# The opening of a two-layer DiT block on one core: who issues the loads, and where the modulation chunks and weight splits stand

## The chip, the cores and the metric

The kernel runs on one core of a Trainium2 chip. The metric is device time in microseconds (us) of one execution; the median of the runs is compared. The core has several engines that run side by side and are held together by semaphores: PE (TensorE, matrix products), DVE (VectorE), ACT (ScalarE), POOL (GpSimd) and SP (SyncE, which here only issues transfers). Sixteen DMA engines move the data. SBUF is the on-chip memory, PSUM holds the results of PE.

## The reference

What is computed is a block of two transformer layers on a sequence `x` (512 tokens of 1024 values) with a context `ctx` (256 tokens), all in fp32. The parts that matter here are those at the very beginning, the modulation and the first layer's mixer:

```python
for i in range(DEPTH):                      # DEPTH = 2
    sh1, sc1, g1, sh2, sc2, g2 = _adaln(c, w_mod[i], b_mod[i])      # silu(c) @ w_mod + b_mod
    hx = _modulate(_rms_norm(x, norm1[i]), sh1, sc1)                # h * (1 + scale) + shift
    # the same for ctx, with c_ctx
    if i == 0:
        yx = _fourier_hyena_mixer(hx, *fh)                          # begins with  proj = h @ w_in
        yc = _fourier_hyena_mixer(hc, *fh)
    else:
        yx = ...                                                    # attention over x and ctx
    x = x + g1 * yx
    x = x + g2 * _conv_ffn(_modulate(_rms_norm(x, norm2[i]), sh2, sc2), *ffn)
```

with

```python
def _rms_norm(x, g):
    y = x32 * lax.rsqrt(jnp.mean(x32 * x32, axis=-1, keepdims=True) + EPS)
    return y * g
```

The mixer also needs a small filter network, three layers of `h = sin(freq * (h @ w + b))`, which depends on no token and is calculated in the opening too.

## The kernel before

All activations are kept transposed: a row tile `x[d]` (d = 0 to 7) holds 128 of the 1024 values on the partitions, and along them 512 tokens of `x` and 256 of `ctx`. A matrix product in fp32 is made of three products of a shorter type: each factor is split into a high part (`hi`, a copy on ACT, L133) and a low part (`lo`, a subtraction on DVE, L138), and `mm3` (L158 to L160) issues high by high, high by low and low by high. A weight tile of 512 KB has its parts `wr` (raw), `wh` and `wl`; a row tile of the normalised input has `hh` and `hl`.

The opening is the part up to the end of the first three projections, about 72 us long. Its order on PE, DVE, SP and ACT is the order in which the code is written (a block in which the scheduler leaves these four engines alone). It has these pieces:

- **Loads**, all issued by SP: the table of columns `pcol` (L189), the constants `cst` (L191), the conditions `cT` (L198), the filter's `zT` and `fw` (L403, L404), eight tiles of `x` of 256 KB (L460), eight of the context of 128 KB (L462), then the modulation's weights `wm`, two chunks of 2 x 1 MB (L209), and three tiles of `w_in` (L146). There are only so many DMA semaphores, so an issue further back can wait for the landing of an earlier load.
- **Silu** of the conditions on ACT (L201), which brings a load of ACT's function table, into `sT`.
- **Sums of squares**: `s1(d)` and `s2(d)` for x and the context, a square on ACT (L267) and an addition on DVE (L274). `f1(True, 0)` and `f2(True, 0)` sum over the partitions with PE (`fold`, L280), scale on DVE (`nrm_s`, L285) and take the reciprocal root in 11 small DVE operations (L167 to L176). `f1(True, 1)` and `f2(True, 1)` spread the result over all partitions with PE (L298) and copy it out on ACT (L301).
- **Modulation chunks**: four chunks of 512 outputs of shift and scale. `gemv_pe` multiplies `sT` with a chunk of weights in 8 matmuls of PE (L219) and copies the result on ACT (L222); the function that it returns, called `turn` below, brings it onto the partitions with four matmuls (L227) and adds the bias on DVE (L232). Chunks 0 and 1 cover the row tiles 0 to 3, chunks 2 and 3 the row tiles 4 to 7. `make_A` (L251) makes of the scale the factor A. The pool of `wm` has two buffers.
- **The filter network**: a matmul (L410), the argument's reduction on DVE (`sine`, L384 to L393) and Sin on ACT (L414).
- **Spare matmuls** (`spare`, L470): products whose result nobody reads, that fill waits of PE.
- **Row tiles**: `both(d, 0)` multiplies x by A and by the root for x and for the context (L308, DVE) and adds the shift (L309, ACT), which gives `hh`; `both(d, 1)` gives `hl` (L313, DVE).
- **Products**: `first(m, k)` is the share of row tile k in projection m, six matmuls. The results of three projections grow side by side in PSUM (`ps3`). After the first four row tiles come the others, one after another, each with three products.

All small results of PE (`ms`) share two PSUM buffers: the fold's, the spreading's, the chunks' and the filter's matmuls all write a buffer of this pair, so that each must wait until the one before the last has been read. From the taps (L616) on nothing is changed.

Of the kernel before, what the change touches and what calls it, by code (L numbers as in the profile page):

```python
# [22 lines left out]
C = 256  # L23
C0 = 514
# [61 lines left out]
class Builder:  # L86
# [94 lines left out]
    def setup(self):  # L181
        nc, I = self.nc, self.I
        self.P0 = self.pool("P0")
        self.W = self.pool("W", bufs=3)
        self.ps = self.pool("psA", space=PSUM)
        self.sm = self.pool("sm", bufs=2)
        p = self.P0
        self.pcol = self.t(p, [P, NCOLS], F32, "pcol")
        nc.sync.dma_start(self.pcol, I["pcol"])  # L189
        cst = self.t(p, [P, 132], F32, "cst")  # L190
        nc.sync.dma_start(cst, I["cst"])  # L191
        self.ident, self.e4, self.sel, self.alt = cst[:, 0:128], cst[:, 128:129], cst[:, 129:131], cst[:, 131:132]
        self.ones32 = self.t(p, [P, 32], F32, "ones32")
        nc.vector.memset(self.ones32, 1.0)
        self.mod = [self.t(p, [P, 48, 2], F32, f"mod{i}") for i in range(2)]
        self.A = [[self.t(p, [P, 2, 8], F32, f"A{i}{k}") for k in range(2)] for i in range(2)]
        cT = self.t(p, [P, KD, 2], F32, "cT")
        nc.sync.dma_start(cT, I["cT"])  # L198
        self.sT = self.t(p, [P, KD, 32], F32, "sT")
        nc.vector.memset(self.sT, 0.0)  # L200
        nc.scalar.activation(self.sT[:, :, 0:2], cT, AF.Silu)  # L201
        self.sbp = self.pool("sbp", side="right")
        self.sb = self.t(self.sbp, [P, 2, D], F32, "sb")

# [191 lines left out]
    def filter_mlp(self):  # L396
# [3 lines left out]
        zT = self.t(p, [66, 384], F32, "zT")  # L400
        fw = self.t(p, [P, 3, P], F32, "fw")
        self.w4 = self.t(p, [P, 1024], F32, "w4")
        nc.sync.dma_start(zT, I["zT"])  # L403
        nc.sync.dma_start(fw, I["fw"])  # L404

        def layer(l, h, step):
            if step == 0:
# [25 lines left out]
    def mixer(self):  # L433
# [21 lines left out]
        with self.tc.manual_schedule(engines={ENG.PE, ENG.DVE, ENG.SP, ENG.Activation}):  # L455
# [3 lines left out]
            for d in range(KD):  # L459
                nc.sync.dma_start(x[d][:, 0:512], I["xT"][d])  # L460
            for d in range(KD):
                nc.sync.dma_start(x[d][:, C0 : C0 + C], I["cxT"][d])  # L462
            wm = [self.gemv_raw(0), self.gemv_raw(1)]
            win = [self.wraw(I["w_in"][m]) for m in range(3)]
            ps3 = [self.mm() for _ in range(3)]
# [10 lines left out]
            for d in range(KD):  # L476
                s2(d)
            f1(True, 0)
            spare(5)
            f2(True, 0)  # L480
            spare(3)
            f1(True, 1)
            g0 = self.gemv_pe(0, 0, wm[0])
            wm.append(self.gemv_raw(2))
            f2(True, 1)
            h = layer(0, layer(0, pa, 1), 2)
            g0()
            spare(3)
            wins = [self.wsplit(win[0])]
            g1 = self.gemv_pe(0, 1, wm[1])  # L490
            spare(1)
            wm.append(self.gemv_raw(3))
            nc.sync.dma_start(self.w4, I["w4"])
            for tt in (4, 5):
                dec[tt] = tp()
                nc.sync.dma_start(dec[tt], I["decay"][tt])
            wins.append(self.wsplit(win[1]))
            g1()
            self.make_A(0, 0, b=4)
            for d in range(KD):  # L500
                hh.append(self.t(hp, [P, TW], F32R, f"hh{d}"))
# [10 lines left out]
                self.proj_k(ps3[m], wins[m], hh, hl, k)  # L512

            pa = layer(1, h, 0)
            spare(5)
            both(0, 0)
            both(1, 0)
            both(0, 1)
            first(0, 0)
            first(1, 0)  # L520
            wins.append(self.wsplit(win[2]))
            both(1, 1)
            both(2, 0)
            first(0, 1)
            first(1, 1)
            both(3, 0)
            both(2, 1)
            first(2, 0)
            first(2, 1)
            g2 = self.gemv_pe(0, 2, wm[2])  # L530
            both(3, 1)
            h = layer(1, layer(1, pa, 1), 2)
            first(0, 2)
            g2()
            first(1, 2)
            first(2, 2)
            g3 = self.gemv_pe(0, 3, wm[3])
            first(0, 3)
            g3()
            self.make_A(0, 0, a=4)  # L540
            first(1, 3)
            first(2, 3)
            self.close("wm")
            self.pg = self.pool("pg")
# [1398 lines left out]
```

## Time and profile before

| what | us |
|---|---|
| median of 3 runs | 1628.01 (1627.53 to 1628.06) |
| the profiled execution, its own time | 1633.3 |
| its span, first to last instruction | 1631.5 |
| busy PE in the span | 1589.6 (97%) |
| busy DVE, ACT | 1048.2 (64%), 620.1 (38%) |
| mean granted clock of PE | 0.991 |
| the first square (L267) starts at | 6.32 |
| the first product of a row tile starts at | 37.31 |
| the first matmul that reads `hl` of row tile 4 starts at | 59.28 |
| the taps (L616) begin at | 72.56 |

The profile is of one execution. A row of a timeline has the start, the time to the end of the group in us, the engine, the line, the operation, what goes out and in, and how many instructions are in the group; in square brackets stands how long the engine was idle before it and what it waited for. A row of the stages has the stretch, its length, and the busy time of each engine with its number of instructions; then the granted clock of PE (1.00 is full speed), the share of the DMA engines' time that was taken, and GB/s. A row of the chain of waits has start, length and what ran. fp32 matmuls that are not split are counted twice in the timeline.

### The profile page before, as it was taken

The page shows a single profiled execution, that of the slowest core. Times are in us where ns is not written, and L with a number is a line of the kernel's source. Part 1 is how long each engine was busy: PE and PEld are TensorE (multiplying, and loading weights), DVE is VectorE, ACT ScalarE, POOL GpSimd, SP SyncE. Part 2 cuts the span into 40 slices and gives each one's busy share as a digit, 9 for nine tenths or more (in the row PEclk, how much of TensorE's full clock was granted, in tenths as well). Part 3 has the DMA queues.
Part 4 walks back from the last instruction along what each step waited for, and adds up shares of the span by engine and source line. Part 5 has one row for each costly group of instructions (what it writes and reads, how often), then busy time and mean ns, then how long its engine had stood idle before and what let it go on. Part 6 is the DMA issues. An engine that isn't in the chain of part 4 may idle for free.

```text
span 1631.5 us, 20800 instructions
## 1 busy us (share of the span) xinstructions
PE 1589.6 (97%) x8248; PEld 1300.2 (80%) x8248; DVE 1048.2 (64%) x1702; ACT 620.1 (38%) x883; POOL 109.5 (7%) x165
## 2 busy tenths in 40 slices
PE   7999998999999999999999999999989999999999
PEld 5687888888888888888888887566559888888887
DVE  5788869878786354643354577899977544344243
ACT  4451224424222212222133337898953432233131
POOL 0112134000000000000000001121210000000000
PEclk9999998999999999999999999999999999999999
DMA  9336412533443243432342210000033232222222
GB/s 344 108 117 211 170 36 72 194 117 106 166 155 129 66 141 129 159 125 71 108 147 99 95 55 16 13 11 13 0 129 116 78 103 102 80 104 98 83 91 90
DMA packets 54542, 173.35 MB, mean 106 GB/s; under 512 B 6188, under 2 KB 9454, under 8 KB 53422
## 3 DMA queue, kind: packets, MB, share of 16 engines
q1 hardware_dynamic: 54445, 172.03, 30.5%
q8 instruction: 65, 1.06, 0.3%
q14 instruction: 32, 0.25, 0.0%
HBM read 166.24 MB, written 5.77 MB: 105 GB/s over the span
## 4 chain that ended last, share of the span: by engine, by line
PE 81%; DVE 13%; DMA 2%; issue 2%; ACT 1%; POOL 1%; SPq 0%; POOLq 0%; ACTq 0%; DVEq 0%
PE mm L158 24%; PE mm L159 23%; PE mm L160 23%; PE pv L1613 2%; DVE junk L243 2%; DVE S L1589 1%; DVE wl L138 1%; PE s L1559 1%; DVE wr L1628 1%; DMA wr<-w_in 1%; PE k L158 1%; PE k L159 1%; PE k L160 1%; DMA wm<-wmod0a 1%; PE mm L616 1%
## 5 line engine op out<-in xcount | busy, mean ns | idle before, releaser
L158 PE MATMUL mm<-hh,wh 128*128 128x512 f32 (+2 forms) x1360 | 480.9, 356 | 1.8 <-ACT wh L133 0.9
L159 PE MATMUL mm<-hl,wh 128*128 128x512 f32 (+2 forms) x1360 | 478.6, 353 | 2.3 <-DVE hl L313 2.3
L160 PE MATMUL mm<-hh,wl 128*128 128x512 f32 (+2 forms) x1360 | 478.4, 352 | 1.6 <-DVE wl L138 1.6
L133 ACT ACTIVATE wh<-wr 128x1024 fp32r<-128x1024 f32 (+1 forms) x192 | 197.8, 1033 | 579.8 <-PE mm L159 544.6
L138 DVE TENSOR_TENSOR wl<-wr,wh 128x1024 fp32r<-128x1024 f32 (+2 forms) x192 | 231.2, 1207 | 234.9 <-ACT wh L133 228.3
L158 PEld LDWEIGHTS mm<-hh,wh 128*128 128x128 f32 x1360 | 256.6, 189 | 48.4 <-issue 7.6
L159 PEld LDWEIGHTS mm<-hl,wh 128*128 128x128 f32 x1360 | 257.1, 189 | 39.2 <-DVE hl L313 3.5
L160 PEld LDWEIGHTS mm<-hh,wl 128*128 128x128 f32 x1360 | 256.9, 189 | 37.5 <-DVE wl L138 2.2
L243 DVE SCALAR_TENSOR_TENSOR junk<-wr,sb 128x1024 bf16<-128x1024 f32 x128 | 156.2, 1220 | 41.2 <-DMA wr<-wmodT 40.7
L158 PE MATMUL mm<-ah,wh 128*128 128x512 f32 (+1 forms) x480 | 172.4, 359 | 0.0
L160 PE MATMUL mm<-ah,wl 128*128 128x512 f32 (+1 forms) x480 | 172.2, 359 | 0.0
L159 PE MATMUL mm<-al,wh 128*128 128x512 f32 (+1 forms) x480 | 171.9, 359 | 0.0
L1143 DVE SCALAR_TENSOR_TENSOR xr<-mm,mod,xr 128x512 f32<-128x512 f32 (+1 forms) x100 | 61.8, 632 | 160.6 <-PE mm L160 160.1
L159 PEld LDWEIGHTS mm<-al,wh 128*128 128x128 f32 x480 | 90.5, 189 | 14.2 <-DVE al L138 0.2
L158 PEld LDWEIGHTS mm<-ah,wh 128*128 128x128 f32 x480 | 90.4, 188 | 14.1 <-issue 0.3
L160 PEld LDWEIGHTS mm<-ah,wl 128*128 128x128 f32 x480 | 90.4, 188 | 14.2
L1613 PE MATMUL pv<-S,V 128*128 128x512 f32 x192 | 93.9, 598 | 2.5 <-ACT S L1592 2.5
L1175 ACT ACTIVATE fg<-fg 128x772 f32<-128x772 f32 (+1 forms) x44 | 32.6, 741 | 98.0 <-DVE fg L375 91.4
L1567 ACT ACTIVATE S<-s,rks 128x512 f32<-128x512 f32 x96 | 62.6, 685 | 12.4 <-PE pv L1613 8.5
L1613 PEld LDWEIGHTS pv<-S,V 128*128 128x128 f32 x192 | 34.5, 190 | 34.7 <-issue 29.3
L1589 DVE TENSOR_TENSOR S<-S,mx 128x1536 f32<-128x1536 f32 x32 | 55.4, 1750 | 2.3 <-POOL mx L1585 2.3
L1585 POOL PARTITION_ALL_REDUCE mx<-mx x16 | 44.9, 2806 | 161.6 <-DVE mx L1582 161.6
(337 smaller groups left out, 2273.2 us busy)
## 6 DMA issues: line engine op xcount, KB each, us to landing
wr<-w_up SPq DMA_DIRECT2D x88, 512.0 KB, 3.2
wr<-wmodT SPq DMA_DIRECT2D x80, 512.0 KB, 3.2
wr<-w_dn SPq DMA_DIRECT2D x32, 512.0 KB, 3.2
wm<-wmod0a SPq DMA_DIRECT2D x8, 1024.0 KB, 8.9
wr<-w_in SPq DMA_DIRECT2D x16, 512.0 KB, 4.2
wr<-w_out SPq DMA_DIRECT2D x13, 512.0 KB, 3.7
wr<-w_dn SPq DMA_DIRECT2D x17, 384.0 KB, 3.0
wr<-w_o SPq DMA_DIRECT2D x11, 512.0 KB, 3.2
```

Source lines behind the costliest of these rows:

```text
L133: self.nc.scalar.activation(dst, src, AF.Copy)
L138: (eng or self.nc.vector).tensor_tensor(dst, src, hi.bitcast(F32), op=ALU.subtract)
L158: mmul(out, wh, xh, start=start, stop=False)
L159: mmul(out, wh, xl, start=False, stop=False)
L160: mmul(out, wl, xh, start=False, stop=stop)
L243: nc.vector.scalar_tensor_tensor(junk, raw, 1.0, self.sb[:, j, :], op0=ALU.mult, op1=ALU.mult, accum_out=acc)
L1143: nc.vector.scalar_tensor_tensor(x[m][:, a2:b2], ps[:, a2:b2], mod[:, 8 * sec + m, c : c + 1], x[m][:, a2:b2], op0=ALU.mult, op1=ALU.add)
L1175: nc.scalar.activation(g[:, :n], g[:, :n], AF.Silu)
L1567: nc.scalar.activation(c.S[a][j // 3][:, j % 3, :], c.ps[a, j], AF.Copy, scale=c.r[:, g : g + 1])
L1585: nc.gpsimd.partition_all_reduce(c.m[a][:, 1, :], c.m[a][:, 0, :], P, bass.bass_isa.ReduceOp.max)
L1589: v.tensor_tensor(c.S[a][h], c.S[a][h], mb.to_broadcast([P, 3, T]), op=ALU.subtract)
L1613: nc.tensor.matmul(c.P[a], V[:, j, o : o + 128], c.S[a][j // 3][:, j % 3, :], start=j == 0, stop=j == 5)
```

## The change

Three things are changed, all in the opening; what is computed is the same.

First, `pcol`, `zT`, `fw` and the eight context tiles are issued by ACT instead of SP, 11 of the loads, and Silu is moved behind these 11 issues. Second, on PE the modulation chunks 0 and 1 are put between the folds and spreadings, with fewer spare matmuls. Third, only the first weight is split ahead of the row tiles; the second and third are split behind row tiles 0 and 2, the row tiles are normalised one by one, and the products are in another order.

```diff
-        nc.sync.dma_start(self.pcol, I["pcol"])
+        nc.scalar.dma_start(self.pcol, I["pcol"])
...
-        nc.scalar.activation(self.sT[:, :, 0:2], cT, AF.Silu)
+        self.cT = cT
...
-        nc.sync.dma_start(zT, I["zT"])
-        nc.sync.dma_start(fw, I["fw"])
+        nc.scalar.dma_start(zT, I["zT"])
+        nc.scalar.dma_start(fw, I["fw"])
...
             for d in range(KD):
-                nc.sync.dma_start(x[d][:, C0 : C0 + C], I["cxT"][d])
+                nc.scalar.dma_start(x[d][:, C0 : C0 + C], I["cxT"][d])
+            nc.scalar.activation(self.sT[:, :, 0:2], self.cT, AF.Silu)
...
             f1(True, 0)
-            spare(5)
-            f2(True, 0)
-            spare(3)
-            f1(True, 1)
+            spare(2)
             g0 = self.gemv_pe(0, 0, wm[0])
             wm.append(self.gemv_raw(2))
+            f1(True, 1)
+            f2(True, 0)
+            g0()
+            g1 = self.gemv_pe(0, 1, wm[1])
+            wm.append(self.gemv_raw(3))
             f2(True, 1)
             h = layer(0, layer(0, pa, 1), 2)
-            g0()
-            spare(3)
+            g1()
             wins = [self.wsplit(win[0])]
-            g1 = self.gemv_pe(0, 1, wm[1])
-            spare(1)
-            wm.append(self.gemv_raw(3))
...
-            wins.append(self.wsplit(win[1]))
-            g1()
             self.make_A(0, 0, b=4)
...
             pa = layer(1, h, 0)
-            spare(5)
+            spare(3)
             both(0, 0)
+            both(0, 1)
+            wins.append(self.wsplit(win[1]))
             both(1, 0)
-            both(0, 1)
             first(0, 0)
+            both(1, 1)
             first(1, 0)
-            wins.append(self.wsplit(win[2]))
-            both(1, 1)
             both(2, 0)
             first(0, 1)
             first(1, 1)
+            both(2, 1)
+            wins.append(self.wsplit(win[2]))
+            first(0, 2)
+            first(1, 2)
             both(3, 0)
-            both(2, 1)
             first(2, 0)
             first(2, 1)
             g2 = self.gemv_pe(0, 2, wm[2])
             both(3, 1)
             h = layer(1, layer(1, pa, 1), 2)
-            first(0, 2)
+            first(2, 2)
             g2()
-            first(1, 2)
-            first(2, 2)
+            first(0, 3)
             g3 = self.gemv_pe(0, 3, wm[3])
-            first(0, 3)
+            first(1, 3)
             g3()
             self.make_A(0, 0, a=4)
-            first(1, 3)
             first(2, 3)
```

The order of the instructions on ACT at its very beginning, before (the numbers behind names tell instances of a tile apart; `s_38` is the first square):

```order
L201 ACT_TABLE_LOAD
L201 ACTIVATE sT_81<-cT_79 128x8x2
L267 ACTIVATE s_38_168<-x_16_109 128x512
L267 ACTIVATE s_39_170<-x_17_110 128x512
L267 ACTIVATE s_40_173<-x_18_111 128x512
```

and now:

```order
L189 DMA pcol_67<-pcol 128x360
L403 DMA zT_119<-zT 66x384
L404 DMA fw_120<-fw 128x384
L462 DMA x_16_108<-cxT 128x256
L462 DMA x_17_109<-cxT 128x256
L462 DMA x_18_110<-cxT 128x256
L462 DMA x_19_111<-cxT 128x256
L462 DMA x_20_112<-cxT 128x256
L462 DMA x_21_113<-cxT 128x256
L462 DMA x_22_114<-cxT 128x256
L462 DMA x_23_115<-cxT 128x256
L463 ACT_TABLE_LOAD
```

Eleven issues stand ahead of the table's load, Silu and the first square.

On PE, from the fold of x (L280 with four columns) to the second chunk's turn (the second L227), before:

```order
L280 MATMUL ms_214<-ones_3_71,s_38_168 128x1 x4
L470 MATMUL mm_157<-s_28_125,cst_69 128x256 x5
L280 MATMUL ms_248<-ones_3_71,s_46_191 128x1 x2
L470 MATMUL mm_157<-s_28_125,cst_69 128x256 x3
L298 MATMUL ms_278<-cst_69,rq_r_241 128x128 x4
L219 MATMUL ms_285<-wm_143,sT_81 32x512 x8
L298 MATMUL ms_299<-cst_69,rq_r_273 128x128 x2
L227 MATMUL ms_314<-cst_69,s_83_294 128x2 x4
L470 MATMUL mm_157<-s_28_125,cst_69 128x256 x3
L219 MATMUL ms_327<-wm_146,sT_81 32x512 x8
L470 MATMUL mm_157<-s_28_125,cst_69 128x256
L227 MATMUL ms_351<-cst_69,s_93_336 128x2 x4
```

and now:

```order
L280 MATMUL ms_214<-ones_3_71,s_38_168 128x1 x4
L471 MATMUL mm_157<-s_28_124,cst_69 128x256 x2
L219 MATMUL ms_245<-wm_143,sT_81 32x512 x8
L298 MATMUL ms_259<-cst_69,rq_r_241 128x128 x4
L280 MATMUL ms_266<-ones_3_71,s_46_191 128x1 x2
L227 MATMUL ms_293<-cst_69,s_68_254 128x2 x4
L219 MATMUL ms_299<-wm_146,sT_81 32x512 x8
L298 MATMUL ms_313<-cst_69,rq_r_291 128x128 x2
L227 MATMUL ms_328<-cst_69,s_87_308 128x2 x4
```

The first chunk comes ahead of the spreading of x, the fold of the context behind that, and no spare matmul stands between the first chunk and the second chunk's turn.

On DVE, from chunk 0's bias (the first L232) to the first row tiles, before:

```order
L232 TENSOR_TENSOR mod_4_73<-ms_314,pcol_67 128x8
L138 TENSOR_TENSOR wl_324<-wr_149,wh_323 128x1024
L138 TENSOR_TENSOR wl_348<-wr_151,wh_347 128x1024
L232 TENSOR_TENSOR mod_4_73<-ms_351,pcol_67 128x8
L251 SCALAR_TENSOR_TENSOR A_6_75<-mod_4_73,pcol_67 128x4 x2
L308 SCALAR_TENSOR_TENSOR s_117_414<-x_16_109,A_6_75,s_81_283 128x512
```

and now:

```order
L232 TENSOR_TENSOR mod_4_73<-ms_328,pcol_67 128x8
L138 TENSOR_TENSOR wl_335<-wr_149,wh_334 128x1024
L251 SCALAR_TENSOR_TENSOR A_6_75<-mod_4_73,pcol_67 128x4 x2
L308 SCALAR_TENSOR_TENSOR s_115_398<-x_16_108,A_6_75,s_71_264 128x512
L308 SCALAR_TENSOR_TENSOR s_116_401<-x_16_108,A_6_75,s_90_316 128x256
L313 SCALAR_TENSOR_TENSOR hl_99_346<-s_115_398,mod_4_73,hh_98_345 128x512
L313 SCALAR_TENSOR_TENSOR hl_99_346<-s_116_401,mod_4_73,hh_98_345 128x256
L138 TENSOR_TENSOR wl_407<-wr_151,wh_406 128x1024
```

The low part of the second weight stands behind the first row tile instead of ahead of it; the first L232 of the second listing is that of chunk 1, and chunk 0's now stands ahead of the filter's `sine`.

## The prediction

> **What bounds the kernel now.** I read the page's head first, then the busy time by stage, then the chain of waits through the opening, and last the timelines of PE, DVE and ACT with the granted clock beside them.
>
> ```profile
> span 1631.5 us, 20800 instructions
> PE 1589.6 (97%) x8248; PEld 1300.2 (80%) x8248; DVE 1048.2 (64%) x1702; ACT 620.1 (38%) x883; POOL 109.5 (7%) x165
> ```
>
> PE is busy for 97% of the span, so 42 us of idle PE are all that any ordering can win. The stages (columns: length, busy PE, PEld, DVE, ACT, POOL, granted clock, DMA share, GB/s) say how much of that lies where the change acts:
>
> ```profile
> 0.00:37.30 37.30, 28.17 (x126) 20.05 (x126) 20.13 (x60) 14.59 (x27) 1.20 (x36) 0.91 0.92 340
> 37.30:59.30 22.00, 19.67 (x122) 14.08 (x122) 16.30 (x32) 8.41 (x15) 4.31 (x2) 1.00 0.62 226
> 59.30:72.50 13.20, 13.20 (x73) 11.34 (x73) 9.05 (x18) 5.02 (x9) 0.00 (x0) 1.00 0.13 40
> ```
>
> The last of them is solid: 13.20 of 13.20 us. The change leaves it as it is, so the whole question is when it begins, that is when the first matmul with hl4 (the low part of row tile 4) starts, 59.28 us before. Every microsecond by which that instant moves is taken over by the span. The chain of waits up to the first product:
>
> ```profile
> 6.30 6.12 DMA x<-xT
> 12.44 1.25 ACT s L267 x3
> ...
> 16.12 4.48 PE mm L470 x10
> ...
> 23.77 0.59 ACT s L301
> ```
>
> The data come first, then squares and sums, then PE. The 4.48 us of L470 are spare matmuls; they lie on this chain because fold and spread stand behind them; then comes the first copy of a spreading, 0.59.
>
> **The loads.** Before, SP issues everything, and ACT starts its squares when x0 lands. The rows are, in this order, ACT's timeline, SP's timeline, the loads by kind (size, median us to landing), the tile x, and the waits of SP's queue:
>
> ```profile
> 3.94 1.28 ACT L201 ACT_TABLE_LOAD   x1 [3.94 <-DMA cT<-cT]
> 5.23 0.22 ACT L201 ACTIVATE sT<-cT 128x16 f32<-128x16 f32 x1
> 6.32 0.63 ACT L267 ACTIVATE s<-x 128x512 f32<-128x512 f32 x1 [0.87 <-DMA x<-xT]
> ...
> 1.17 0.42 SPq L191 DMA_DIRECT2D cst<-cst  x1
> ...
> cT<-cT SPq DMA_DIRECT2D x1, 8.0 KB, 2.2
> ...
> x<-cxT SPq DMA_DIRECT2D x8, 128.0 KB, 4.2
> ...
> DMA to landing us min/median/max: 3.0/4.8/6.1
> ...
> SPq L462 <- DMA x<-xT: 2.6, 7, 0.7
> ```
>
> Afterwards 11 issues stand on ACT ahead of its table load, Silu and squares. The last row says that issues wait for earlier landings (here 7 times): a load is let out only when the one whose place it takes has landed. In the built program the ACT issue of cx2 (the third context tile's load) waits for cT, and that of cx7 for cx2. cT is now SP's second load, issued when cst was (1.17), so it lands at 1.17 + 2.2 = 3.4. cx2 goes out by 3.7, lands 4.2 later at 7.9, cx7's issue ends by 8.25, and table load and Silu (1.28 + 0.22) come after that. The first square starts at 9.75 instead of 6.32. With the fastest and slowest landing of an x load (3.0 and 6.1, the row with minimum, median and maximum) it is 8.55 or 11.6. The issue time saved on SP (11 issues at about 0.4) buys nothing here, since the queue that needs the data waits behind its own issues.
>
> The Trainium skill's "DMA: Bandwidth & Descriptors", section "Issuing engines are not separate DMA queues", says that issuing from several engines saves only the sequencer's issue time, the transfers sharing the same 16 DMA engines. The trace agrees: 0.92 of the DMA engines' time is taken over the whole first stage.
>
> **Sums.** By 9.75 most tiles have landed, so from there DVE sets the pace:
>
> ```profile
> 9.72 8.19 DVE L274 TENSOR_TENSOR s<-s,s 128x512 f32<-128x512 f32 x13 [0.31 <-ACT s L267]
> 17.83 0.15 DVE L285 TENSOR_SCALAR nrm_s<-ms 128x4 f32<-128x4 f32 x1
> ...
> 20.00 0.16 DVE L176 SCALAR_TENSOR_TENSOR rq_r<-rq_b,rq_r 128x4 f32<-128x4 f32 x1
> ```
>
> The first add can start when two squares are done (0.63 each, overlapping a little), about 10.94, the second some 0.8 later at 11.74. The other 13, as the row has them, took 8.11 us to the next instruction (9.72 to 17.83), so nrm_s of x starts at about 19.85 instead of 17.83: two microseconds late. If DVE ran them closer together, gemv 0 (the first modulation chunk) would still have to wait for its 2 MB: up to the end of that chunk 5.8 MB are to be moved, and the 340 GB/s of the first stage, with a start near 3 us, give 17 + 3 = 20 us. The reciprocal root takes 2.33 us as before (17.83 to 20.16).
>
> **The chunks between sums and spreadings.** These rows price the new order (x16 is 8 matmuls of the program, each twice):
>
> ```profile
> 22.68 1.05 PE L298 MATMUL ms<-cst,rq_r 128*128 128x128 f32 x8
> 24.41 1.92 PE L219 MATMUL ms<-wm,sT 128*32 128x512 f32 x16 [0.67 <-ACT s L301]
> ...
> 27.04 0.71 PE L298 MATMUL ms<-cst,rq_r 128*128 128x128 f32 x4 [0.70 <-ACT s L222]
> 28.21 1.05 PE L227 MATMUL ms<-cst,s 128*128 128x2 f32 x8 [0.46 <-ACT s L301]
> ...
> 24.44 0.67 DVE L384 TENSOR_SCALAR s<-ms,pcol 128x384 f32<-128x384 f32 x1
> ...
> 27.71 0.36 DVE L393 TENSOR_SCALAR s<-s 128x384 f32<-128x384 f32 x1
> ...
> 29.67 1.23 DVE L138 TENSOR_TENSOR wl<-wr,wh 128x1024 fp32r<-128x1024 f32 x1 [0.20 <-ACT wh L133]
> ...
> 35.75 2.21 DVE L308 SCALAR_TENSOR_TENSOR s<-x,A,s 128x512 f32<-128x512 f32 x4
> ...
> 37.31 0.49 PE L158 MATMUL mm<-hh,wh 128*128 128x512 f32 x1
> ```
>
> ms, the PSUM tile that all these matmuls write, has two buffers, so each of these steps waits for the reader of the last but one. gemv 0 waits for nrm_s of x: 20.05 to 21.97. Its copy lasts 0.6; spread x (1.05) stands behind it, 22.7 to 23.7; fold c waits for spread x's copy, 24.4 to 24.95 (four matmuls that I price a little under the 0.71 of spread c). DVE's root for c ends at 27.3 and chunk 0's addition at 27.5; only that frees the buffer for gemv 1, 27.5 to 29.5. Copy, spread c (0.71), copy, and turn 1 (1.05) reach 32.4. Behind DVE's sine (3.63 before, from 24.44 to the end of L393 at 28.07) comes wh of weight 0, to 32.85, and wl of weight 0 (1.23), to 34.1; A is ready at 34.5. From the start of L308 to the first product it was 1.56 us (35.75 to 37.31), so the first product comes at 36.2: **1.1 us earlier**, in spite of the two lost at the front. The gain is that the second weight's split and 12 of the 25 spares are off the path.
>
> **Projections.** The splits that were ahead are now between row tiles, on DVE:
>
> ```profile
> 39.59 0.40 PE L158 MATMUL mm<-hh,wh 128*128 128x512 f32 x1
> ...
> 40.65 0.39 PE L158 MATMUL mm<-hh,wh 128*128 128x512 f32 x1
> ...
> 45.82 1.92 PE L219 MATMUL ms<-wm,sT 128*32 128x512 f32 x16
> ...
> 54.97 0.95 PE L227 MATMUL ms<-cst,s 128*128 128x2 f32 x8
> ...
> 59.28 0.50 PE L159 MATMUL mm<-hl,wh 128*128 128x512 f32 x1 [0.86 <-DVE hl L313]
> ```
>
> One product (six matmuls) is 39.59 to 40.65, 1.06 us. On DVE, each pair of L308 is about 1.1 (2.21 for two), each pair of L313, of the same shape, is taken at as much, and wl of weight 1 is 1.23; three row tiles need 34.6 + 6 x 1.1 + 1.23 and some waits for ACT's hh, and the first six products end near 45.1 instead of just before 45.82 (-0.75). From there to chunk 3's turn stand five products instead of four: +1.06. The turn comes at 55.2 (54.97 before), and hl4's first matmul 4.31 later, as now: 59.6. **At full clock the sum is +0.3 us.** That turn now has one product behind it instead of two, so PE's stall there grows by 1.06.
>
> **The clock.** The granted clock is where I expect the rest (PE's wait before fold x, and stretches with the same columns as the stages):
>
> ```profile
> 14.45 1.67 PE L280 MATMUL ms<-ones,s 128*128 128x1 f32 x8 [1.91 <-DVE s L274]
> ...
> 11.30:14.70 3.40, 1.49 (x9) 1.01 (x7) 3.07 (x5) 3.31 (x9) 0.00 (x0) 1.00 0.98 313
> 14.70:18.10 3.40, 3.40 (x13) 3.04 (x13) 2.74 (x9) 1.10 (x3) 0.00 (x0) 0.50 0.93 355
> 57.00:60.40 3.40, 2.54 (x14) 2.00 (x13) 3.40 (x8) 2.74 (x6) 0.00 (x0) 1.00 0.00 0
> 188.80:192.20 3.40, 1.51 (x10) 1.22 (x10) 2.48 (x6) 1.38 (x2) 1.57 (x2) 1.00 0.42 154
> 192.20:195.60 3.40, 3.40 (x13) 2.93 (x12) 3.37 (x7) 1.36 (x2) 0.00 (x0) 0.50 0.19 42
> ```
>
> Two stretches of 3.4 us in which PE was busy for 1.49 and 1.51 us are each followed by one at half the clock, though PE was wholly busy there; after 2.54 it stays at 1.00, as the solid stage from 59.30 on shows. Somewhere between lies the point at which it is lost. Three places fall under it now. (a) Spares end near 12.5 (14.45 - 1.91), fold x is at 16.5: idle 3.9 us where it was 1.9, and only 2 spares follow instead of 5 before the next wait. The clock is lost as before, but gemv 0 (1.92) comes while it may still be away: between 0 and 1.9, I take 1.0, half of it. (b) Between gemv 0's end and gemv 1's start PE works 1.05 + 0.55 + 1.0 = 2.6 of 5.5 us, a share of 47%, against 44% in the two stretches that lost it and 75% in the one that kept it. At half clock gemv 1 costs 1.9 more, spread c 0.5, turn 1 0.65: 0 to 3.05, I take 1.0, since a stretch may end between them. (c) At chunk 3's stall busy falls from 2.54 to 2.54 - 1.06 = 1.5, as in the two stretches that lost it; a solid stretch of 3.4 us at half the clock does 1.7 us less work: 0 to 1.7, I take 1.7, as the row at 192.20 shows. Sum: 0.3 + 1.0 + 1.0 + 1.7 = **+4.0 us**.
>
> The Trainium skill's "TensorE: Matmul & The Clock Gate", section "Why this matters for your kernels", asks for no idle gaps of PE over about 3 us and says that one idle window halves the rate. By it only (a), 3.9 us, would cost, an estimate of +1.3 in all. The trace is stricter: 1.91 us of idle before fold x was followed by half clock.
>
> The profiled execution took 1633.3 us around its span of 1631.5 (1.8 lie outside), 5.3 over the median of the runs, 1628.01. The opening lies in both alike, so 1633.3 + 4.0 = 1637.3 in a profile and **1632.0** as median.
>
> **The rivals.** *The clock keeps* at (b) and (c), or comes back before gemv 1: then +0.3 to +1.3, 1628.3 to 1629.3, no change. For it: windows may fall so that a stall is split between two, as the 2.54 were; against it: the rows at 188.80. Chance 0.33. *ACT's queue comes free early*: cx2 lands in 3.0, the first square starts at 8.55, 1.2 earlier than I take, and the clock keeps; then 0.3 - 1.2 = -0.9, 1627.1, not slower than before. It decides where the sums are the last thing gemv 0 waits for; against it, the 5.8 MB above hold gemv 0 to about 20. Chance 0.08, and I leave 0.06 for a gain over 0.2%, that is 3.3 us: hl4 would have to be there by 56.0, while the PE work from the first product on (nine products, two chunks, two turns: some 15 us at full clock, plus the DVE waits of the row tiles) hardly allows it. *The second queue doesn't help and hurts more*: the slowest landing, 6.1, puts 1.85 on top, and all three clock terms at their upper end give 0.3 + 1.9 + 3.05 + 1.7 = 7, 1635; chance 0.1, part of the forecast's side.
>
> **How the numbers follow.** A measurement of this kernel can tell about 0.2%, 3.3 us, from no change. The forecast, two or three of the clock terms, has 0.43, and with the worst case 0.53; of that a little falls short of 3.3 us. Keeping the clock (0.33) and an early ACT (0.08) are both within. So slower 0.54, same 0.40, faster 0.06. The likeliest case's own range is 1630.5 to 1635; to hold eight in ten it reaches to the early ACT, 1627, and to the worst sum with a little of the late landing, 1635.5.
>
> **What would show it.** Right, if in the profile afterwards the first square starts at 9 to 10 us, nrm_s of x near 19.9, gemv 1 after 27 behind chunk 0's L232, the first product near 36 to 38, the wait before hl4's first matmul near 1.9 us, and a stretch of clock 0.5 after 60. Wrong, if the squares start by 7.5 (the issues don't hold ACT), if the clock stays at 1.00 from 21 us on, or if hl4 is there before 58. A change of more than 1 us behind 72.5 would say that I missed a later effect.

## The result

The changed kernel is slower: 1640.94 us (1639.12 to 1642.09, 4 runs) against 1628.03 us (1627.53 to 1629.07, 4 runs) for the kernel before; the ratio is 1.0075, with a 95% interval of 1.0062 to 1.0088. The forecast had the sign, but 1632.0 and not more than 1635.5: it saw 4 of 12.9 us.

The head of the page and the stages of the forecast, now of the changed kernel (columns as before):

```profile
span 1640.3 us, 20754 instructions
...
PE 1589.0 (97%) x8224; PEld 1295.3 (79%) x8224; DVE 1048.4 (64%) x1702; ACT 619.6 (38%) x883; POOL 108.1 (7%) x165
```

```profile
0.00:37.30 37.30, 22.37 (x86) 13.03 (x86) 15.78 (x52) 10.41 (x23) 1.20 (x36) 0.77 0.85 315
37.30:59.30 22.00, 17.53 (x95) 12.32 (x96) 18.24 (x30) 8.76 (x15) 2.88 (x2) 1.00 0.70 255
59.30:72.50 13.20, 11.49 (x58) 8.26 (x57) 8.28 (x19) 5.65 (x11) 0.00 (x0) 0.79 0.19 49
```

PE did less work in the first 37 us (22.37 against 28.17 us) at a lower granted clock (0.77 against 0.91), and the stretch that was solid before has waits and a clock of 0.79. To see where time goes, it is better to cut at the same events in both: the fold of x, the first product of a row tile, chunk 2 (gemv 2), hl4's first matmul, the taps. First the kernel before, then the changed one, in windows cut at these events:

```profile
14.45:37.31 22.86, 20.82 (x108) 14.75 (x109) 14.44 (x47) 6.68 (x13) 0.00 (x0) 0.85 0.98 391
37.31:45.82 8.51, 7.04 (x37) 5.59 (x37) 7.83 (x15) 4.54 (x8) 1.49 (x1) 1.00 1.01 352
45.82:59.28 13.46, 12.60 (x87) 8.47 (x86) 8.44 (x18) 3.84 (x7) 2.81 (x2) 1.00 0.38 147
59.28:72.56 13.28, 13.28 (x74) 11.36 (x74) 9.07 (x18) 5.04 (x9) 0.00 (x0) 1.00 0.13 40
```

```profile
17.65:41.64 23.99, 18.45 (x85) 10.25 (x85) 12.74 (x46) 4.73 (x10) 0.00 (x0) 0.64 0.84 341
41.64:55.17 13.53, 10.30 (x48) 7.46 (x48) 11.94 (x16) 5.62 (x9) 2.88 (x2) 1.00 0.81 286
55.17:67.56 12.39, 10.69 (x74) 6.62 (x73) 6.97 (x18) 3.84 (x7) 0.00 (x0) 0.97 0.09 27
67.56:83.67 16.11, 16.11 (x74) 13.69 (x74) 9.07 (x18) 5.04 (x9) 0.00 (x0) 0.81 0.13 34
```

The fold comes 3.20 us later (17.65 for 14.45). From there to the first product it is 1.13 longer, though 12 spare matmuls are gone, at a clock of 0.64. The products up to chunk 2 take 5.02 longer (two products more are in there, 2.12; of the other 2.9, 1.76 is idle PE, 3.23 us against 1.47, and the rest are matmuls that run less closely behind a wait, 0.50 each instead of 0.40). Chunks 2 and 3 are 1.07 shorter, one product having gone ahead, and the last stretch, the same work, is 2.83 longer at a clock of 0.81. The sum is 11.11, which is how much later the taps begin (83.67 for 72.56). Behind the taps both kernels do the same: 1640.3 - 83.67 = 1556.6 us and 1631.5 - 72.56 = 1558.9.

How the steps between fold and first product follow one another is in PE's timeline of the changed kernel; in brackets stands how long PE was idle and what it waited for:

```profile
17.65 1.05 PE L280 MATMUL ms<-ones,s 128*128 128x1 f32 x8 [3.72 <-DVE s L274]
...
21.28 3.64 PE L219 MATMUL ms<-wm,sT 128*32 128x512 f32 x16 [1.23 <-issue]
25.61 2.07 PE L298 MATMUL ms<-cst,rq_r 128*128 128x128 f32 x8 [0.69 <-ACT s L222]
28.36 1.01 PE L280 MATMUL ms<-ones,s 128*128 128x1 f32 x4 [0.68 <-ACT s L301]
29.63 1.87 PE L227 MATMUL ms<-cst,s 128*128 128x2 f32 x8 [0.25 <-DVE nrm_s L285]
31.88 3.64 PE L219 MATMUL ms<-wm,sT 128*32 128x512 f32 x16 [0.38 <-DVE mod L232]
```

Every step waits for the one that reads the result of the step just ahead: chunk 0 begins when nrm_s has read the fold's (DVE's L285, 21.02 to 21.17); spread x waits for chunk 0's copy, the fold of the context for spread x's copy, the turn for nrm_s, chunk 1 for chunk 0's bias. Both chunks take 3.64 us instead of 1.92: half clock for the whole stretch.

And the loads, in the chain of waits of the changed kernel:

```profile
1.17 3.09 DMA cT<-cT
4.28 0.34 ACTq L462
4.66 4.74 DMA x<-cxT
```

That is the path the forecast named (cT lands, cx2 is issued, cx2 lands, cx7 is issued), each landing somewhat longer: 3.09 and 4.74 instead of 2.2 and 4.2.

### The profile page after: what moved, and what is told of

The parts are those of the page before. It is cut to its first block, busy times and chain, and to the rows that moved or that the text cites. A ratio compares the mean times of both kernels' runs of the same rounds, so it can differ in the third digit from the quotient of the medians.

```text
span 1640.3 us, 20754 instructions
## 1 busy us (share of the span) xinstructions
PE 1589.0 (97%) x8224; PEld 1295.3 (79%) x8224; DVE 1048.4 (64%) x1702; ACT 619.6 (38%) x883; POOL 108.1 (7%) x165
## 4 chain that ended last, share of the span: by engine, by line
PE 79%; DVE 15%; issue 2%; ACT 1%; DMA 1%; POOL 1%; POOLq 0%; ACTq 0%; SPq 0%; DVEq 0%
PE mm L158 23%; PE mm L159 23%; PE mm L160 23%; PE pv L1611 2%; DVE junk L243 2%; DVE wl L138 2%; DVE S L1587 1%; PE s L1557 1%; DVE wr L1626 1%; DVE hl L313 1%; PE ms L219 1%; PE k L158 1%; PE k L160 1%; PE k L159 1%; PE mm L614 1%
```

## The experiments

The instants of each profile (us) and the times:

| kernel | first product | hl4's first matmul | taps | median | ratio to before, 95% |
|---|---|---|---|---|---|
| before | 37.31 | 59.28 | 72.56 | 1628.03 | |
| before, second profile | 35.69 | 57.66 | 70.94 | 1629.31 (one run) | |
| changed | 41.64 | 67.56 | 83.67 | 1640.94 | 1.0062 to 1.0088 |
| changed, loads as before | 39.27 | 66.24 | 79.51 | 1641.08 | 1.0047 to 1.0094 |
| loads alone | 40.39 | 62.36 | 75.64 | 1634.08 | 1.0019 to 1.0040 |
| chunks alone | 42.68 | 67.11 | 80.40 | 1638.34 | 1.0039 to 1.0076 |
| splits and products alone | 33.16 | 57.42 | 70.69 | 1632.45 | 1.0005 to 1.0029 |
| changed, more spares | 37.92 | 64.50 | 77.79 | 1638.92 | 1.0050 to 1.0080 |
| changed, sine first | 34.61 | 59.90 | 73.20 | 1633.88 | 1.0018 to 1.0043 |
| changed, w4 later | 40.18 | 64.17 | 79.00 | 1639.19 | 1.0055 to 1.0088 |
| changed, chunk 3 earlier | 43.86 | 68.80 | 82.08 | 1639.52 | 1.0056 to 1.0086 |
| changed, all mended | 33.75 | 56.77 | 70.06 | 1628.41 | 0.9988 to 1.0006 |
| before, three loads | 33.99 | 55.96 | 69.24 | 1627.62 | 0.9987 to 1.0005 |
| before, L384 early | 33.76 | 55.73 | 69.02 | 1626.76 | 0.9979 to 0.9996 |

The instants are those of one execution each, and it can lie off the median: the profiled one took 1642.09 us of the changed kernel, 1630.60 with the sine first, 1629.25 with splits and products alone, 1637.29 with w4 later and 1628.91 with L384 early. The ratios are to the kernel before, measured beside each (medians 1628.0 to 1629.8). In all of these profiles the part from the taps to the end is 1555.6 to 1559.1 us long, so whatever the change does, it does ahead of the taps.

### The change with its loads undone

```diff
-        nc.scalar.dma_start(self.pcol, I["pcol"])
+        nc.sync.dma_start(self.pcol, I["pcol"])
...
-                nc.scalar.dma_start(x[d][:, C0 : C0 + C], I["cxT"][d])
-            nc.scalar.activation(self.sT[:, :, 0:2], self.cT, AF.Silu)
+                nc.sync.dma_start(x[d][:, C0 : C0 + C], I["cxT"][d])
```

(`zT` and `fw` alike; Silu back at its place.)

> The change with its first part undone: all loads are issued by SP again and Silu stands where it stood; chunks, splits and products stay as changed. Theory 1 (the late squares cost the time: they open the 3.7 us gap ahead of the fold, and with it the half clock up to 35 us): first square at 6.3 us, nrm_s of x near 18, no half clock behind 22, first product by 38, time 1629 to 1632. Theory 2 (the new order of PE with its 13 spares loses the clock by itself): gemv 0 to gemv 1 still run at half clock, 1634 to 1638. Theory 3 (most is lost among the row tiles): 8 products and the wait of hl4 keep their length, 1634 to 1636 with a full clock before 35.

The time did not move: 1641.08, slower even than theory 2 had it. Theory 1 falls. The fold of x is back at 13.80, but what comes next now waits for something else, in PE's timeline:

```profile
19.68 1.93 PE L219 MATMUL ms<-wm,sT 128*32 128x512 f32 x8 [3.85 <-DMA wm<-wmod0a]
22.04 1.80 PE L219 MATMUL ms<-wm,sT 128*32 128x512 f32 x8 [0.43 <-DMA wm<-wmod0a]
```

Chunk 0 stands ahead of spread x, so PE idles 3.85 us for its weights; they are there at 19.7 and 22.0, however early the sums are. With the loads on ACT, chunk 0 begins at 21.28: in that order the late squares are mostly hidden behind the weights.

### The loads alone

The same lines, on the kernel before.

> The kernel before with the first part of the change alone: pcol, zT, fw and the eight context tiles issued by ACT, Silu behind them. Theory 1: first square near 11, nrm_s of x near 21, time 1632 to 1636. Theories 2 and 3: the spare matmuls and the old order take most of the delay up, 1628 to 1631.

1634.08, which is 4.3 us slower than the kernel before beside it (1629.78; by the interval 3.1 to 6.5). In stages:

```profile
17.53:40.39 22.86, 20.82 (x108) 14.73 (x109) 14.44 (x47) 6.39 (x13) 0.00 (x0) 0.85 0.85 336
40.39:48.90 8.51, 7.04 (x37) 5.58 (x37) 7.83 (x11) 3.59 (x6) 3.11 (x2) 1.00 1.00 344
```

These stages are as long as those of the first profile of before, to the hundredth; all is 3.08 us later (17.53 for 14.45). So the loads by themselves cost what the sums are late (nrm_s of x at 20.90 for 17.83), and the spares take nothing of it up. Theory 1 is right about this part alone, and wrong as an account of the whole.

### The chunks alone

On the kernel before, the lines of the diff from `f1(True, 0)` to `g1()`: chunks 0 and 1 between folds and spreadings, 2 spares there instead of 12.

> The kernel before with the second part alone: chunks 0 and 1 between the folds and spreadings, with fewer spares; loads on SP, both weights split ahead of the row tiles, products in the old order. Theory 1: no slower than before, 1625 to 1629. Theory 2: half clock between 20 and 33 us and 1632 to 1636. Theory 3: 1627 to 1630.

1638.34, slower by 8.6 us: theory 2, and more than it had. The stage from fold to first product:

```profile
14.12:42.68 28.56, 23.38 (x88) 13.96 (x89) 14.76 (x49) 7.14 (x14) 0.00 (x0) 0.52 0.94 380
```

28.56 us instead of 22.86, with a clock of 0.52 over all of it.

### Splits and products alone

On the kernel before, the row tiles one by one, the second and third weight split behind tiles 0 and 2, the new order of products.

> The kernel before with the third part alone: second and third weight split behind row tiles 0 and 2, row tiles one by one, products in the new order, so that chunk 3's turn has one product behind it. Theories 1 and 2: about the sum of the full clock, 1627 to 1629, with 1.7 on top if the stall ahead of hl4 loses the clock. Theory 3: 1632 to 1635, with the first eight products 2 us or more longer than before and the half clock behind hl4.

1632.45, between the theories: 2.7 us slower than before (by the interval 0.8 to 4.7), with the half clock neither ahead of the products nor behind hl4 in the profile:

```profile
33.16:45.03 11.87, 10.27 (x50) 7.33 (x49) 10.67 (x14) 4.66 (x8) 3.46 (x2) 1.00 1.01 394
45.03:57.42 12.39, 10.69 (x75) 6.63 (x74) 8.06 (x20) 4.79 (x9) 0.00 (x0) 1.00 0.26 91
```

From the first product to hl4 it takes 24.26 us (11.87 + 12.39) where the kernel before takes 21.97 (8.51 + 13.46): 2.3 us more at full clock. The forecast had 1.4 for this (23.4, from 36.2 to 59.6). The profile's taps (70.69) are earlier than in the profiles of before: here the clock was kept from the start (1.00 from the fold to the first product), and one weight's split is out of the way of the first product. But this was the fastest of ten executions; the median says more than that one execution.

The three parts alone cost 4.3, 8.6 and 2.7, in all 15.6, and together 12.9: what the loads cost is in part hidden by the chunks' wait for their weights.

### More spares

On the changed kernel, 20 spare matmuls more (the text below says 17; its own list, 7, 3 and 10, and the diff make 20).

```diff
-            spare(8)
+            spare(15)
...
-            spare(2)
+            spare(5)
             g0 = self.gemv_pe(0, 0, wm[0])
             wm.append(self.gemv_raw(2))
+            spare(2)
             f1(True, 1)
+            spare(1)
             f2(True, 0)
+            spare(1)
             g0()
+            spare(4)
             g1 = self.gemv_pe(0, 1, wm[1])
             wm.append(self.gemv_raw(3))
+            spare(2)
```

> The changed kernel with 17 more spare matmuls that fill PE's waits (15 instead of 8 ahead of the fold of x, 5 instead of 2 behind it, and 2, 1, 1, 4 and 2 between the steps up to the second chunk's turn). Theory 2a (the new order costs because its thin work loses the clock): full clock from 22 us on, gemv 1 at 1.9 us instead of 3.6, first product by 38 instead of 41.6, time 1634 to 1637. Theory 2b (the order itself is slow: all small results go through one PSUM buffer, since the filter's first result holds the other until the sine, which now stands behind chunk 0's bias, so every step waits for the reader of the step before): the clock may keep, but the first product stays at 40 or later, 1638 to 1641.

```profile
17.91:37.92 20.01, 17.86 (x110) 12.27 (x110) 12.74 (x46) 4.37 (x9) 0.00 (x0) 1.00 1.00 407
37.92:52.13 14.21, 11.25 (x48) 8.70 (x48) 12.99 (x18) 5.72 (x9) 2.60 (x2) 0.88 0.78 275
```

The clock is 1.00 up to the first product, which comes at 37.92, as theory 2a has it, and not at 40, as 2b does: half clock is worth 23.99 - 20.01 = 4.0 us there. Then the clock is lost among the row tiles (0.88). The median, 1638.92, is 2 us below the changed kernel's, with intervals that overlap; the spares don't mend it, so 2a is part of the cause and not the whole.

### The filter's sine first

On the changed kernel, the first sine on DVE ahead of the sums.

```diff
             spare(8)
+            pa = layer(0, pa, 1)
...
-            h = layer(0, layer(0, pa, 1), 2)
+            h = layer(0, pa, 2)
```

> The changed kernel with the filter's first sine on DVE ahead of the sums (DVE is idle there up to 12 us), so that the filter's result gives its PSUM buffer back before the fold of x. Nothing else is moved. Theory 2b: gemv 0 no longer waits for nrm_s of x and gemv 1 no longer for chunk 0's bias; from the fold of x (17.7) to the second chunk's turn (38.5) it is 3 to 6 us shorter, 1634 to 1637. Theory 2a: gemv 0 and gemv 1 stay at half clock (3.6 us each) and the gain is the sine's 3.6 us on DVE at most, of which PE sees 1 or less: 1639 to 1641.

1633.88: of the 12.9 us, 7 are gone with this one edit, and the interval is clear of the changed kernel's. PE's timeline:

```profile
21.77 2.90 PE L219 MATMUL ms<-wm,sT 128*32 128x512 f32 x16
24.60 1.16 PE L298 MATMUL ms<-cst,rq_r 128*128 128x128 f32 x8
25.60 0.50 PE L280 MATMUL ms<-ones,s 128*128 128x1 f32 x4
26.36 1.05 PE L227 MATMUL ms<-cst,s 128*128 128x2 f32 x8 [0.25 <-DVE nrm_s L285]
27.34 1.92 PE L219 MATMUL ms<-wm,sT 128*32 128x512 f32 x16
```

The waits in brackets are gone but one; chunk 1 begins 4.5 us earlier and no longer waits for chunk 0's bias. The filter's first result is there by 8.5 us in the changed kernel and is read by L384, the sine's first operation; until then it holds one of the two buffers of `ms`. Before, L384 stood behind the second reciprocal root (24.44); the change puts it behind chunk 0's bias (31.75), and the steps of PE up to chunk 1 go through the other buffer one at a time. With two buffers they follow closely, and PE, busy, gets its clock back: from fold to first product 16.55 us at 0.83 instead of 23.99 at 0.64. This experiment takes away waits and thin work (short steps with waits between them) together, so it doesn't split them; that 20.01 us remain with the clock kept and the single buffer says that, in these two profiles, at least 3.5 are the buffer's. L384 alone was not tried on the changed kernel; but the sine's other operations were hardly in the way there, since DVE, done with them at 35.4, waited 3.12 us for turn 1.

### w4 later

```diff
-            nc.sync.dma_start(self.w4, I["w4"])
...
             both(3, 1)
+            nc.scalar.dma_start(self.w4, I["w4"])
```

> The changed kernel with the load of w4 (the filter's last weights) issued by ACT behind row tile 3 instead of by SP ahead of the row tiles, so that POOL's two operations on it (L423, L424) fall behind the fourth row tile and not beside row tile 1. If POOL's work beside it is what stretched L313 of row tile 1 to 3.07 us (1.15 elsewhere), that row goes back to 1.15 and the first eight products end 2 us earlier: 1638 to 1639.5. If not, the row stays long wherever POOL runs and the time stays at 1640 to 1641.5.

In the changed kernel the second pair of L313 (hl of row tile 1) had

```profile
44.11 1.14 DVE L308 SCALAR_TENSOR_TENSOR s<-x,A,s 128x512 f32<-128x512 f32 x2
45.65 3.07 DVE L313 SCALAR_TENSOR_TENSOR hl<-s,mod,hh 128x512 fp32r<-128x512 f32 x2 [0.40 <-ACT hh L309]
```

on DVE, and POOL, just then,

```profile
45.48 1.27 POOL L423 TENSOR_TENSOR s<-w 128x512 f32<-128x512 f32 x1 [43.76 <-DMA w<-w]
46.83 1.61 POOL L424 TENSOR_TENSOR w<-w 128x512 f32<-128x512 f32 x1
```

With w4 later, POOL runs at 57.50, that pair takes 1.15, and the stage of products is

```profile
40.18:51.78 11.60, 10.28 (x49) 7.51 (x48) 10.01 (x16) 5.61 (x9) 0.00 (x0) 0.97 0.84 284
```

1.93 us shorter than 13.53. The median is 1.75 lower, as expected, though the intervals overlap. The Trainium skill's "GPSIMD Engine Reference", section "Specifications", offers a cause: POOL shares its SBUF interfaces with VectorE, and contends there with instructions of DVE that run in a 2-port mode or have two SBUF inputs. L313 has two (s and hh), and this trace agrees: 3.07 beside POOL, 1.15 away from it. Two inputs are not the whole condition: in the profile of before, L387, with one, took 1.33 beside POOL and 0.36 elsewhere, and no view here shows an instruction's mode.

### Chunk 3 one product earlier

```diff
-            first(0, 3)
             g3 = self.gemv_pe(0, 3, wm[3])
-            first(1, 3)
+            first(0, 3)
             g3()
             self.make_A(0, 0, a=4)
+            first(1, 3)
             first(2, 3)
```

> The changed kernel with chunk 3 one product earlier, so that two products instead of one stand behind its turn, as before the change. If the longer stall there is what loses the clock behind hl4: full clock from 60 to 75 us, hl4's first matmul 1.06 us earlier, the taps 2.5 to 4 us earlier than 83.7, time 1637 to 1639. If the clock is lost by the earlier stalls, hl4's first matmul is 1 us earlier and the clock behind it is as the position of the stretches has it: 1639 to 1641.

```profile
57.58:68.80 11.22, 10.36 (x74) 6.62 (x73) 5.96 (x16) 3.83 (x7) 0.00 (x0) 1.00 0.09 26
68.80:82.08 13.28, 13.28 (x73) 11.36 (x73) 9.08 (x18) 5.04 (x9) 0.00 (x0) 1.00 0.14 39
```

Chunks 2 and 3 take 1.17 less and the stretch behind hl4 is back at full clock, 13.28 for 16.11. But this execution lost more ahead of the products (first product at 43.86), and the median, 1639.52, isn't told from the changed kernel's. Nor does the half clock behind hl4 always come: with the loads undone, with more spares, with the sine first and with the third part alone, the same stall was followed by 13.27 to 13.30 us; with w4 later it came (14.83). So the stall puts the clock at risk; it isn't a fixed price.

### The kernel before, a second profile

> The kernel before, unchanged, profiled a second time. If its half clock from 14.7 to 21.5 us, on which the forecast was built, is there in every execution, the taps begin again near 72.6 us. If it comes and goes with the wait ahead of the fold of x (1.91 us in the profile that the forecast had, 0.51 in that of the third part alone, which stayed at full clock), the taps begin at 69 to 70 us with the clock kept.

```profile
14.47:35.69 21.22, 19.18 (x109) 13.22 (x109) 14.37 (x47) 6.88 (x13) 0.00 (x0) 0.92 1.00 405
```

It lies between: the wait ahead of the fold was 1.16, the clock in this stage 0.92 and not 0.85, the taps at 70.94. In the three-loads kernel, whose PE program is that of before, with a wait of 0.59, the clock is 1.00 and the taps begin at 69.24. The profile that the forecast went by was one of the worse executions of the kernel before.

### The kernel before with L384 early

```diff
             spare(8)
+            pa = self.sine_arg(pa, self.col("fb1"))     # L384 alone: the operation that reads PSUM
...
-            h = layer(0, layer(0, pa, 1), 2)
+            h = layer(0, layer(0, pa, 11), 2)           # the other six, where they were
```

> The kernel before with the first of the sine's seven operations on DVE (L384, the one that reads PSUM) ahead of the sums, so that the filter's result gives its PSUM buffer back at 8 us instead of 25; the other six stay. If the single buffer costs the kernel before too: the fold of the context, spread x and gemv 0 come earlier, the first product 1 to 2 us earlier, 1626 to 1627. If the landing of the modulation's weights (about 21 us) and of the first w_in tile (26 us) is what sets the pace there: 1628 to 1629.5, no change.

1626.76, ratio 0.9988 with an interval of 0.9979 to 0.9996: about 2 us faster than before, and the only kernel here that is. The single buffer cost the kernel before, too:

```profile
20.60 1.05 PE L298 MATMUL ms<-cst,rq_r 128*128 128x128 f32 x8
21.58 1.92 PE L219 MATMUL ms<-wm,sT 128*32 128x512 f32 x16
23.43 0.71 PE L298 MATMUL ms<-cst,rq_r 128*128 128x128 f32 x4
24.21 1.05 PE L227 MATMUL ms<-cst,s 128*128 128x2 f32 x8
```

The waits of 0.67, 0.70 and 0.46 between these four steps are gone.

### Everything mended

The changed kernel with loads and Silu as before, L384 early, 8 spares behind the fold of x, w4 later and chunk 3 earlier.

> The changed kernel with everything mended that the runs so far put a price on: loads and Silu as before, L384 ahead of the sums, 8 instead of 2 spare matmuls behind the fold of x, the load of w4 issued behind row tile 3, chunk 3 one product earlier. If these explain the whole loss: as fast as before or faster, 1626 to 1629, first product at 32 to 34 us. If the row tiles one by one cost by themselves (2.7 us in the third part alone): 1630 to 1632.

```profile
14.47:33.75 19.28, 18.00 (x96) 12.03 (x97) 11.95 (x45) 5.83 (x12) 0.00 (x0) 0.82 1.01 415
33.75:45.36 11.61, 9.97 (x50) 7.42 (x49) 10.01 (x16) 5.63 (x9) 0.00 (x0) 1.00 0.94 370
```

1628.41, ratio 0.9997 (0.9988 to 1.0006): no slower than before. The five mends together make up for the whole loss, though one of them, L384 early, gains 2 us on the kernel before, too; against that kernel (1626.76) this one is 1.7 us slower, with intervals that overlap. What is left of the change, the order of chunks and of row tiles, gains nothing: the first product is at 33.75, as with L384 early alone (33.76), and the row tiles then take their longer way.

### Three loads on ACT

On the kernel before, only `pcol`, `zT` and `fw` on ACT, Silu right behind them, the context tiles on SP.

> The kernel before with only pcol, zT and fw issued by ACT and Silu right behind these three; the context tiles stay on SP. If the eight context issues are what holds ACT: the first square comes at 5.5 to 6 us, SP reaches x0 1.3 us earlier, nrm_s of x 0.5 to 1 us earlier, 1626.5 to 1628.5. If any issue on ACT ahead of the squares costs: the first square after 7 us and 1629 or more.

The first square came at 6.11 (6.32 before), nrm_s of x at 16.80, and the time is 1627.62, ratio 0.9996 (0.9987 to 1.0005): no change that can be told. So it isn't issuing on ACT that costs, but the eight context issues, which wait for landings while ACT has squares to do. The gain of the earlier sums does not reach the end for sure either.

## Why the prediction was right or wrong

**The loads: right, and undersized.** The chain cT, cx2, cx7, table load, Silu, square is what happened; the first square was at 10.95 and not 9.75, since the two landings took 3.09 and 4.74. nrm_s of x was at 21.02 and not 19.85: again 1.2 late. The bound given for a slow landing (11.6) held. Inside the whole change this part costs little, as the run with the loads undone shows (1641.08): chunk 0 then waits for its weights. The forecast had that bound, "20 us" for the first chunk's 2 MB, and the weights came at 19.7 and 22.0.

**The chunks at full clock: right.** From the fold to the first product the sum had 19.7 us (16.5 to 36.2); with the clock kept by spares it took 20.01; single steps were up to 0.9 late (chunk 1 begins 11.9 us behind the fold, not 11.0), and the steps behind turn 1 took that back in part. But the sentence that gave the reason, like the one on `ms` in the description of the kernel, was wrong: it said that each step waits for the reader of the last but one, and took waits for the reader of the last. The latter is what the trace shows, and the reason is the filter's first result, which holds the other buffer until L384. Because it was taken as given, the forecast did not ask what the change does to L384, which is where 7 of the 12.9 us could be had back.

**The clock: right in kind, the largest term that was mis-sized.** At (a) and (b) the forecast took 1.0 each of at most 1.9 and 3.05. Measured: half clock from the first chunk to the end of the second, 4.0 us by the comparison with more spares. The window of the changed kernel over both chunks:

```profile
21.30:35.50 14.20, 12.20 (x52) 5.71 (x52) 7.08 (x31) 1.17 (x2) 0.00 (x0) 0.50 0.80 335
```

The error is in "half of it": PE was busy for 12.20 of these 14.20 us and yet at 0.50 throughout. So spread x (2.07 for 1.05), the fold of the context (1.01, and 0.61 at full clock with w4 later) and turn 0 (1.87 for 1.05), which the forecast had at full clock, ran at half clock as well; spread c (0.71) and turn 1 (1.05), which it had at half, ran at full. Between the steps stand waits of 0.25 to 0.69 us. Such waits alone do not keep the clock away. With w4 later the order of PE up to there is the same, and the steps between the chunks ran at full clock in spite of them:

```profile
22.10 2.80 PE L219 MATMUL ms<-wm,sT 128*32 128x512 f32 x16
25.62 1.16 PE L298 MATMUL ms<-cst,rq_r 128*128 128x128 f32 x8 [0.71 <-ACT s L222]
27.45 0.61 PE L280 MATMUL ms<-ones,s 128*128 128x1 f32 x4 [0.68 <-ACT s L301]
28.31 1.05 PE L227 MATMUL ms<-cst,s 128*128 128x2 f32 x8 [0.25 <-DVE nrm_s L285]
30.56 3.51 PE L219 MATMUL ms<-wm,sT 128*32 128x512 f32 x16 [1.20 <-DVE mod L232]
```

There the clock came back and was lost again for chunk 1, which is what (b) describes. Chunk 1 ran at half clock (3.51 to 3.64) in every profile with these thin steps ahead of it, and at full (1.92) where spares filled the waits or the freed buffer took them away. Why the changed kernel, unlike the one with w4 later, did not get its clock back in between stays open. For (c), 1.7 was forecast; it was 2.83 in the profile of the change, and nothing in four of the variants.

**The row tiles: wrong.** The sum had 11.0 us from the first product to chunk 2; it was 13.53. POOL's work on w4 took 1.93 of it, and the other 0.6 stays with w4 later (11.60). That work was in the profile of before as well (DVE's L387 with 1.33 us instead of 0.36), where it fell on the sine, which nobody waited for. The change moved row tile 1 into its place. The forecast put POOL at nothing there.

**The base: wrong.** "The opening lies in both alike" does not hold. The 5.3 us by which the profile of before lay above its median were partly a half clock in this very opening, of which the second profile has less (0.92 against 0.85, taps 1.6 us earlier) and that of the three loads none (1.00, taps at 69.24, with nrm_s of x 1.0 earlier as well); the loads alone, with a wait of 4.35 ahead of the fold, had as much (0.85). Another 2.3 lay behind the taps (1558.9 against 1556.6). The changed kernel lost the clock ahead of the first product in its profile and in the two variants with the same order up to there (0.73 with w4 later, 0.53 with chunk 3 earlier). Against the second profile of before the taps are 83.67 - 70.94 = 12.7 us later, and the medians differ by 12.9.

In the profiles the terms add up: 1.2 for the fold, 2.3 up to the first product, 2.5 for the row tiles and 1.1 behind hl4 are the 7.1 us between the forecast's +4.0 and the +11.1 of the two profiles; the base is the other 1.8 of the 12.9. Of the 2.3, 2.0 is the clock at (a) and (b), 4.0 where 2.0 was taken. So the steps of the prediction that failed are the size of the clock terms (2.0 and 1.1 short), the row tiles with POOL's work put at nothing (2.5), the late landings (1.2) and the base (1.8).

Of the rivals, the one that kept the clock, and the one with ACT free early, did not happen; the worst sum, given 0.1, had the late landing and the clock terms at their upper ends and was still 6 us short, without the row tiles and the base.

## What to carry to other kernels

Before moving a step past others, look for what it reads: an operation that frees a small shared buffer belongs as early as its input allows, even if its result is needed late. Here one of seven operations, moved to where its engine was idle, is worth 2 us to the kernel before, and, with the sine's other six, 7 of the 12.9 us that the change lost. And when a term depends on the clock, a single profile is one draw: ask whether the base it is subtracted from has lost the clock in that place, too.

## What the runs showed of the hardware

Whether the clock is lost is not a matter of one wait's length. With PE idle ahead of the fold for 0.51, 0.59 and 1.29 us, the clock stayed at 1.00; 1.16, 1.91 and 3.72 were followed by half clock, and the same stall ahead of hl4 was followed by half clock in two profiles and by full clock in four. Nor does PE's busy time in a stretch settle it: in the changed kernel, at half clock, 3.41 us with PE busy for 2.71 (22.56 to 25.97) were followed by half clock, and 3.41 us with 2.72 (32.80 to 36.21) by full clock. The Trainium skill's "TensorE: Matmul & The Clock Gate", section "What's actually happening", says that PE's activity is watched in windows of about 3.4 us that run freely and do not start with the kernel. These traces agree in the length: half clock lasted 3.4 us in the second profile of before (15.5 to 18.9), 6.8 in the first (14.7 to 21.5) and 17.1 in the changed kernel (19.15 to 36.21), once, twice and five times 3.4. The Trainium skill's advice on the same page, section "Why this matters for your kernels", to avoid idle gaps of over about 3 us is too mild for this kernel: in one execution half clock followed 1.16 us.
